# The second parts of the feed-forward weights w1 and w3, made by an adding DMA in place of a VectorE subtraction

## The chip, the core and the metric

The kernel runs on one core of one Trainium2 chip. The metric is the device time of one execution in microseconds (us). Before the change it is 2998.93 us, the median of three runs (2995.76 to 2999.79). Engines are named as the profile names them: PE is TensorE (PEld its weight loads), DVE is VectorE, ACT is ScalarE, POOL is GpSimd, SP is SyncE.

## The reference

The program computes two hybrid attention layers and then two layers of feed-forward, HGRN2 mixer with pooling, cross-attention and feed-forward, for 512 tokens of 1024 features in float32. The change touches only the feed-forward blocks, of which there are four (`ffn1` and `ffn2` of each of the two later layers). With 2816 hidden features each of them computes:

```python
def swiglu(h, w1, w3, w2):
    return (jax.nn.silu(h @ w1) * (h @ w3)) @ w2

x = x + 0.5 * swiglu(rmsnorm(x, g), w1, w3, w2)
```

## The kernel before, in words

Activations are feature-major: features on the 128 partitions, the 512 tokens on the free axis. A dense product keeps float32 accuracy with three TensorE passes. Every operand is split into a leading part of 12 significant bits (`hi`, type float32r) and the rest (`lo`), and `mm3` (lines 296 to 298) multiplies hi by hi, hi by lo and lo by hi. So every weight that comes from HBM has to be split on the chip. `chunk` does that: it loads a piece with a DMA on SP's queue into one of four buffers `wraw`, ACT copies it into `whi` (line 287, the copy rounds to float32r), and DVE writes `wlo` = piece minus `whi` (line 288). `whi` and `wlo` have two buffers each, so a chunk can be split only when the chunk two before it has been multiplied.

In `ffn`, the weights w1 and w3 lie together: a chunk holds 128 columns of w1 and 128 of w3 for all 1024 input features, 128 x 2048 elements, loaded and split in two pieces of 128 x 1024 (512 KB each). Each block runs in two halves of 11 such chunks; each half ends with 8 chunks of w2. A chunk of w1 and w3 feeds two units (banks of PSUM, three of which rotate under the name `mm`): the first is h @ w1, the second h @ w3, of 24 matmuls of 512 columns each, 48 for a chunk. `ev` evacuates them: DVE scales the first (`si`, line 886), POOL clamps it (line 501), ACT makes a sigmoid of it (lines 504 to 506), POOL multiplies (lines 888, 889), DVE multiplies the second unit with the outcome (`sb`, line 893), and ACT and DVE split that into `hh` and `hl` (lines 256, 257) for the product with w2. At the beginning of a block the row norm is worked out as well (`rt`, lines 440 to 444), which the first `si` needs.

The order of the instructions of each engine is set by the tile framework's scheduler. Every engine takes its instructions in that order, so one that waits holds back all that are behind it. `parts_of` asks for the next unit's weights ahead of the unit that is running.

Of the kernel before, what the change touches and what calls it, by code (L numbers as in the profile page):

```python
"""Two hybrid attention layers, then two HGRN2 / pool / cross-attention layers, on one core.

Activations live feature-major: features on the partitions, the 512 tokens on the free axis.
Dense products run on the tensor engine as float32r passes: an operand is split exactly into
a leading part of 12 significant bits and the rest, and three passes carry lead*lead, rest*lead
and lead*rest, which keeps the accuracy of a float32 product.
"""
# [14 lines left out]
ALU = mybir.AluOpType  # L22
# [14 lines left out]
# tiles of a tag get their room in program order, so work that runs at its own pace has a tag of its own  # L37
# [18 lines left out]
# engines of the steps that more than one can take: V(ector), P(ool), A(ctivation)  # L56
# [7 lines left out]
# ---------------------------------------------------------------- layout of the inputs (host)  # L64
def _chunks(w, c):
    """[K, M] -> [M/c, 128, K/128, c]"""
    k, m = w.shape
    return np.ascontiguousarray(w.reshape(k // P, P, m // c, c).transpose(2, 1, 0, 3))


def _cols(v):
    """[n*128] -> [128, n]"""
    return v.reshape(-1, P).T
# [37 lines left out]
def _constants():  # L111
    a = np.zeros((P, CONST.n), np.float32)

    def put(name, v):
        o, w = CONST.at[name]
        a[:, o:o + w] = v

    p = np.arange(P)[:, None]
    put("ident", np.eye(P))
    put("ones", 1.0)  # L120
    put("bd", (p // 64 == np.arange(P)[None] // 64))
    u = np.arange(512)[None]
    dist = p + 384 - u
    put("causal", np.where(dist >= 0, 0.0, BIG))
    cnt = ((dist >= 0) & (dist <= 128)) * 1 + ((dist >= 0) & (dist % 4 == 0)) * 1 + ((dist >= 0) & (dist % 16 == 0)) * 1
    put("dil", np.where(cnt > 0, -np.log(np.maximum(cnt, 1)), BIG))
    put("tri", (u >= p))
    put("reset", (u % 64 != 0))
    put("diag", p % 32 == np.arange(32)[None])
    t16 = np.arange(16)[None]  # L130
    put("pool", np.concatenate([1.0 / np.minimum(t16 + 1, w) for w in (2, 4, 8, 16)], 1))
    put("eps", EPS)
    # pairs s, t of 32 tokens in the two halves of a segment of 2 hs tokens
    lev = np.zeros((P, 5, 32), np.float32)
    s, t = np.arange(P)[:, None] % 32, np.arange(32)[None]
    for n, hs in enumerate((16, 8, 4, 2, 1)):
        lev[:, n] = (s // (2 * hs) == t // (2 * hs)) & (s % (2 * hs) < hs) & (t % (2 * hs) >= hs)
    sel = np.zeros((96, 8, P), np.float32)
    for h in range(8):
        for part in range(3):  # L140
            sel[32 * part + h, h] = 1.0
    return a, lev, sel


def _pack(i):
# [5 lines left out]
    # 8 frequencies x 16 blocks of 32 tokens  # L151
# [55 lines left out]
# ---------------------------------------------------------------- the program  # L207
class Prog:
# [9 lines left out]
    # tiles  # L218
# [34 lines left out]
    # exact split of float32 into two float32r parts  # L253
# [19 lines left out]
    def chunk(self, ap, kt, c):  # L273
        """One chunk of a weight: both parts, [128, kt, c]."""
# [7 lines left out]
        for o in range(0, n, step):  # L282
            e = min(o + step, n)
            raw = early[o // step] if early else self.raw(flat[:, o:e])
            for a in range(o, e, step // 2 if early else step):
                b = a + step // 2 if early else e
                nc.scalar.activation(hi[:, a:b], raw[:, a - o:b - o], AF.Copy)  # L287
                nc.vector.tensor_tensor(lo[:, a:b], raw[:, a - o:b - o], hi.bitcast(F32)[:, a:b], op=ALU.subtract)  # L288
# [3 lines left out]
    def mm3(self, ps, pairs, first=True, last=True):  # L292
        """ps = sum over pairs of (stationary hi, lo), (moving hi, lo)."""
# [6 lines left out]
    class Unit:  # L300
        """Work of the tensor engine in parts that other work can go between; prep loads its weights."""
# [4 lines left out]
    def weights(self, ap, kt, c):  # L306
        held = []

        def prep():
            if not held:  # L310
                held.extend(self.chunk(ap, kt, c))
# [4 lines left out]
    def unit(self, prep, kt, n, pair, evac, wait=2):  # L316
        """One bank of a dense product: the sum over kt pairs of operands."""
# [16 lines left out]
    def dense(self, chunks, kt, c, act, evac, m0=0, n=T, quick=False):  # L334
        """Feature-major product, a unit for every 128 columns of the weight (one bank); quick: the last ones evacuated at once."""
        units = []
        for ci, ap in enumerate(chunks):
            prep = self.weights(ap, kt, c)
# [8 lines left out]
    def dense_tok(self, chunks, kt, c, act, evac, nb, c0=0):  # L347
        """Token-major product: tokens on the partitions, the weight's columns on the free axis."""
# [9 lines left out]
    def later(self, n, f):  # L358
        """Run f after n more dense units."""
        self.queue.append([n, f])  # L360

    def chain(self, *steps):
        """Steps that hand over between engines, one after each dense unit, so that none waits in its queue."""
# [16 lines left out]
    def parts_of(self, units):  # L380
        """The parts of the units in order, each with its cost; the next unit's weights are loaded ahead."""
# [13 lines left out]
    def weave(self, main, fill, keep=0, lead=0):  # L395
        """Both lists in their order, merged in proportion to their cost; lead of fill's go first, keep last."""
# [14 lines left out]
    # root mean squares  # L411
    def parts(self, sq, hi, n=T, eng=None):
        """The rest of sq beside its leading part hi."""
# [4 lines left out]
    def colsum(self, ps, which, sq, n=T):  # L418
        """ps = which^T sq, which of zeros and minus ones, sq in parts."""
# [16 lines left out]
    def rsqrt(self, ps, n_mean, n=T):  # L436
        """1 / sqrt(-ps / n_mean + EPS): a table value and a Newton step."""
# [9 lines left out]
    class Next:  # L447
        """The operand of the phase after this one, built tile by tile as x gets final."""
# [39 lines left out]
    def norm(self, cur, cols=False, wait=2):  # L488
        """rstd of the tokens, emitted behind the first dense units, which need it only in their evacuation."""
# [8 lines left out]
    def sigmoid(self, x, t, clamp):  # L498
        """t = 1 / (1 + exp(-x)) as exp(-ln(1 + exp(-x))), x held above -40."""
# [10 lines left out]
    def gate(self, ps, r, then):  # L510
        """g = silu(ps * r), then(g)."""
# [5 lines left out]
    # ------------------------------------------------------------ start  # L517
# [50 lines left out]
    def setup_rope(self):  # L568
        """cos and signed sin of the angles, in a dense layout and then in their rows; reduced by multiples of 2 pi in exact parts."""
# [35 lines left out]
    # ------------------------------------------------------------ hybrid layer  # L605
    def qk_tile(self, ps, r, g, rope, done):
        """Head-wise rms norm (two heads a tile), gain, and the rotary part."""
# [33 lines left out]
    def softmax_rows(self, ps, n, mask, P_out):  # L641
        """P_out = softmax of -(ps + mask) along the free axis."""
# [8 lines left out]
    def stack(self, get, st):  # L651
        """Queries and keys of a pair of heads in parts, stacked so that one pass over 128 rows carries two products:
        [qh; qh] and [ql; ql] against [kh; kl]."""
# [18 lines left out]
    def head(self, get, st, hh, h, fox, done):  # L672
        """One head in three stages; rows 64*hh.. of the output bank get it, feature-major."""
# [6 lines left out]
        def scores(i):  # L680
            qh, ql, kk = st[hh]
            n = (i + 1) * P
            # a float32r product at full rate has at least 256 columns
# [34 lines left out]
    def pipeline(self, heads, stacks):  # L718
        """The heads' steps, those of neighbours overlapped; a pair's operands are stacked ahead of it.

        The values of a pair fill the two halves of the tensor engine's columns side by side.
        """
# [18 lines left out]
    def hybrid(self, l, cur, nx):  # L741
# [5 lines left out]
        # tiles: kb 0-3, qb 4-7, ka 8-11, qa 12-15; queries carry -1/8  # L747
# [10 lines left out]
        def ev_va(c, b, ps):  # L758
            # the first 8 columns are the forget gates
# [86 lines left out]
    def forget(self, z):  # L846
        """Running sums of the log forget gates, split into bfloat16 parts."""
# [4 lines left out]
        # log1p(e) = ln(u) + (e - (u - 1)) / u with u = 1 + e  # L852
# [19 lines left out]
    # ------------------------------------------------------------ second block  # L872
    def ffn(self, l, name, cur, nx):
# [4 lines left out]
        for half in range(2):  # L878
# [18 lines left out]
            self.go(self.dense([w13[NH * half + i] for i in range(NH)], KD, 256, xs, ev))  # L897
# [11 lines left out]
    def lower_bound(self):  # L909
        """Per channel of layer 1: lb, 1 - lb and their logs."""  # L910
# [23 lines left out]
    def hgrn_head(self, l, h, f, v, done):  # L934
        """One head as a list of steps, each ready when the one before it is through its engines.

        The decay exp(b_t - b_s), b the running sum of log f, is a product of two factors of at
        most 1 through a token between s and t: for a segment of 2 hs tokens, t in its right and
        s in its left half, that token is the left half's last. Segments of 2 .. 512 tokens
        cover every pair, and the pair t = s has no decay.  # L940
        """
# [29 lines left out]
        def bound():  # L971
            # logaddexp(log lb, log(1 - lb) + log_sigmoid(z)), k = (1 - lb) * sigmoid(-z)
# [19 lines left out]
        def q64():  # L992
            self.on("qe").tensor_tensor(g["qe"], g["qe"], f[4 + h], op=ALU.mult)
            nc.scalar.activation(g["dk"], g["dk"], AF.Exp)
            # decays of whole 64-token chunks, to the middle of 256 and of 512 tokens
# [137 lines left out]
    def mix(self, l, cur, nx):  # L1133
# [26 lines left out]
        def ev_gu(m, ps):  # L1160
# [19 lines left out]
            # the mean over the window minus the frame  # L1180
# [35 lines left out]
    def mem_kv(self, l):  # L1216
        """Keys (feature-major) and values (token-major) of the memory, as units."""
# [27 lines left out]
    def cross(self, l, cur, nx):  # L1245
# [64 lines left out]
        # the first units of the last product run between the steps of the last heads  # L1310
# [74 lines left out]
```

## Time and profile before

| | |
|---|---|
| time, median of 3 runs | 2998.93 us (2995.76 to 2999.79) |
| span of the profiled execution, first to last instruction | 2992.6 us |
| median less that span: what lies around it | 6.3 us |
| PE busy | 2929.1 us (98%) |
| DVE busy | 1674.1 us (56%) |
| ACT busy | 1406.6 us (47%) |
| POOL busy | 745.2 us (25%) |
| DMA, mean | 95 GB/s, 284.10 MB |
| granted TensorE clock, mean | 0.994 |

The profile gives busy times and the span of one execution; its time with what lies around is not listed apart, so the median of the runs stands for it. In rows of groups of instructions the columns are: line, engine, operation, output<-inputs, shapes, count | busy us, mean ns of one | idle us of the engine before them, and what ended most of that idle time. In rows of a timeline the first number is the start in us from the span's beginning, the second the duration in us; a bracket gives the idle time before and what ended it.

### The profile page before, as it was taken

The numbers are of one execution on the slowest core, as the hardware profiler recorded it, in microseconds if no ns is written. First come the engines' busy times: TensorE is split into PE (matmuls) and PEld (weight loads), VectorE is DVE, ScalarE is ACT, GpSimd is POOL, SyncE is SP. The second block draws the span as 40 slices with busy tenths as digits, with TensorE's granted clock in tenths as the row PEclk, the third lists the DMA queues.
The fourth block names the chain that finished last, engine by engine and source line by source line (L and its number), as shares of the span: only waits on it lengthen the run. The fifth ranks groups of instructions, "written<-read, shape, count | busy, mean of one in ns | idle before, by whom it ended". The sixth has DMA issues, their size and how long they took to land.

```text
span 2992.6 us, 39832 instructions
## 1 busy us (share of the span) xinstructions
PE 2929.1 (98%) x15544; PEld 2372.5 (79%) x15544; DVE 1674.1 (56%) x2698; ACT 1406.6 (47%) x2334; POOL 745.2 (25%) x613
## 2 busy tenths in 40 slices
PE   7999999999999999999999999999999999999997
PEld 6777877778788887798888888888888798888886
DVE  7976678766533337785643333433347976643333
ACT  5876467664532434464443233432434654443342
POOL 3101131011331323331032132321323330132231
PEclk9999999999999999999999999999999999999999
DMA  4432233322223232243132323223232242232322
GB/s 159 121 103 82 95 113 94 106 80 94 96 80 107 87 96 89 68 131 99 57 99 79 111 90 99 97 76 111 83 107 83 79 134 85 71 98 79 110 75 76
DMA packets 93436, 284.10 MB, mean 95 GB/s; under 512 B 12656, under 2 KB 13056, under 8 KB 93120
## 3 DMA queue, kind: packets, MB, share of 16 engines
q1 hardware_dynamic: 92928, 281.26, 29.5%
q8 instruction: 122, 2.00, 0.3%
q14 instruction: 66, 0.54, 0.1%
q10 hardware_dynamic: 288, 0.28, 0.0%
q0 software_dynamic: 32, 0.02, 0.0%
HBM read 261.46 MB, written 2.10 MB: 88 GB/s over the span
## 4 chain that ended last, share of the span: by engine, by line
PE 86%; DVE 7%; ACT 2%; issue 1%; POOL 0%; DMA 0%; DVEq 0%; ACTq 0%; POOLq 0%
PE mm L296 27%; PE mm L297 26%; PE mm L298 26%; PE po L712 2%; DVE wlo L288 1%; PE pt L701 1%; PE aux L687 1%; PE aux L421 1%; PE aux L688 1%; PE po L1103 0%; PE aux L296 0%; PE aux L298 0%; PE aux L297 0%; ACT whi L287 0%; DVE hw L1020 0%
## 5 line engine op out<-in xcount | busy, mean ns | idle before, releaser
L296 PE MATMUL mm<-xsh,whi 128*128 128x512 f32 x2304 | 926.9, 403 | 16.9 <-DVE pol L263 8.1
L297 PE MATMUL mm<-xsl,whi 128*128 128x512 f32 x2304 | 910.5, 395 | 8.0 <-DVE xsl L263 7.6
L298 PE MATMUL mm<-xsh,wlo 128*128 128x512 f32 x2304 | 911.2, 396 | 0.0
L287 ACT ACTIVATE whi<-wraw 128x1024 fp32r<-128x1024 f32 (+4 forms) x526 | 498.5, 984 | 572.2 <-PE mm L297 408.0
L288 DVE TENSOR_TENSOR wlo<-wraw,whi 128x1024 fp32r<-128x1024 f32 (+4 forms) x526 | 596.5, 1165 | 110.4 <-ACT whi L287 106.2
L296 PEld LDWEIGHTS mm<-xsh,whi 128*128 128x128 f32 x2304 | 435.6, 189 | 128.4 <-issue 13.1
L297 PEld LDWEIGHTS mm<-xsl,whi 128*128 128x128 f32 x2304 | 435.7, 189 | 108.2 <-DVE xsl L263 14.5
L298 PEld LDWEIGHTS mm<-xsh,wlo 128*128 128x128 f32 x2304 | 435.1, 189 | 101.4 <-DVE wlo L288 0.2
L501 POOL TENSOR_SCALAR sb<-si 128x512 f32<-128x512 f32 x88 | 130.8, 1487 | 770.0 <-DVE si L886 770.0
L433 POOL TENSOR_TENSOR sq<-sq,sq 128x512 f32<-128x512 f32 (+1 forms) x97 | 132.0, 1361 | 722.5 <-ACT sq L430 711.0
L893 DVE TENSOR_TENSOR sb<-mm,sb 128x512 f32<-128x512 f32 x88 | 60.9, 692 | 435.2 <-POOL sb L889 435.2
L297 PE MATMUL mm<-hl,whi 128*128 128x512 f32 x704 | 277.4, 394 | 0.0
L296 PE MATMUL mm<-hh,whi 128*128 128x512 f32 x704 | 277.2, 394 | 0.0
L298 PE MATMUL mm<-hh,wlo 128*128 128x512 f32 x704 | 276.7, 393 | 0.0
L504 ACT ACTIVATE sb<-sb 128x512 f32<-128x512 f32 x88 | 55.8, 634 | 464.1 <-POOL sb L501 464.1
L901 DVE SCALAR_TENSOR_TENSOR x<-mm,x 128x512 f32<-128x512 f32 x64 | 44.3, 692 | 306.7 <-PE mm L298 306.7
L297 PEld LDWEIGHTS mm<-hl,whi 128*128 128x128 f32 x704 | 132.3, 188 | 30.8
L296 PEld LDWEIGHTS mm<-hh,whi 128*128 128x128 f32 x704 | 131.8, 187 | 31.3
L298 PEld LDWEIGHTS mm<-hh,wlo 128*128 128x128 f32 x704 | 132.5, 188 | 30.3
L886 DVE TENSOR_TENSOR si<-mm,rt 128x512 f32<-128x512 f32 x88 | 60.9, 692 | 134.4 <-PE mm L298 134.2
L889 POOL TENSOR_TENSOR sb<-sb,si 128x512 f32<-128x512 f32 x88 | 113.9, 1296 | 67.3 <-ACT sb L506 67.3
L888 POOL TENSOR_TENSOR si<-si,rt 128x512 f32<-128x512 f32 x88 | 114.9, 1306 | 7.3
(360 smaller groups left out, 4580.8 us busy)
## 6 DMA issues: line engine op xcount, KB each, us to landing
wraw<-in_ffn_w_dram SPq DMA_DIRECT2D x176, 512.0 KB
wraw<-in_ffn_w_dram SPq DMA_DIRECT2D x64, 384.0 KB
wraw<-in_ffn_w_dram SPq DMA_DIRECT2D x64, 320.0 KB
z<-z SPq DMA_DIRECT2D x128, 128.0 KB
wraw<-in_w_out_dram SPq DMA_DIRECT2D x32, 512.0 KB
wraw<-in_w_qk_dram SPq DMA_DIRECT2D x30, 512.0 KB
wraw<-in_w_g_dram SPq DMA_DIRECT2D x16, 512.0 KB
wraw<-in_w_gate_dram SPq DMA_DIRECT2D x16, 512.0 KB
```

The costliest lines, as they stand in the source:

```text
L287: nc.scalar.activation(hi[:, a:b], raw[:, a - o:b - o], AF.Copy)
L288: nc.vector.tensor_tensor(lo[:, a:b], raw[:, a - o:b - o], hi.bitcast(F32)[:, a:b], op=ALU.subtract)
L296: self.nc.tensor.matmul(ps, ah, bh, start=first and i == 0, stop=False)
L297: self.nc.tensor.matmul(ps, ah, bl, start=False, stop=False)
L298: self.nc.tensor.matmul(ps, al, bh, start=False, stop=last and i == n - 1)
L433: (eng or self.on("acc")).tensor_tensor(acc[:, :n], acc[:, :n], sq[:, :n], op=ALU.add)
L501: clamp.tensor_scalar(t, x, -40.0, None, op0=ALU.max)
L712: nc.tensor.matmul(self.po[rows, j * P:], v[j][:, 64 * h:64 * h + 64], ptS[b][:, o:o + T - j * P], start=j == 0, stop=j == 2)
L886: nc.vector.tensor_tensor(s, ps, r["r"], op=ALU.mult)
L888: nc.gpsimd.tensor_tensor(s, s, r["r"], op=ALU.mult)
L889: nc.gpsimd.tensor_tensor(b, b, s, op=ALU.mult)
L893: nc.vector.tensor_tensor(b, ps, b, op=ALU.mult)
```

## The change

`chunk` gets a flag `added`, which `ffn` sets for its w1 and w3 chunks from the third of every half on (9 of 11). For these, ACT writes `wlo` = minus the leading part (a copy with scale -1 that rounds to float32r), a DMA issued by POOL adds the same piece of the weight from HBM to `wlo`, and ACT writes `whi` as before. The subtraction of DVE is not there for them. 4 blocks x 2 halves x 9 chunks x 2 pieces make 144 pieces. The other lines of the diff take comments and docstrings out; lines from 288 on stand five numbers later in the changed kernel.

```diff
@@ -270,8 +270,8 @@
-    def chunk(self, ap, kt, c):
+    def chunk(self, ap, kt, c, added=False):
...
@@ -284,13 +284,18 @@
             raw = early[o // step] if early else self.raw(flat[:, o:e])
             for a in range(o, e, step // 2 if early else step):
                 b = a + step // 2 if early else e
+                if added:
+                    nc.scalar.activation(lo[:, a:b], raw[:, a - o:b - o], AF.Copy, scale=-1.0)
+                    nc.gpsimd.dma_start(out=lo[:, a:b], in_=flat[:, a:b], accum_op=ALU.add)
+                    nc.scalar.activation(hi[:, a:b], raw[:, a - o:b - o], AF.Copy)
+                    continue
                 nc.scalar.activation(hi[:, a:b], raw[:, a - o:b - o], AF.Copy)
                 nc.vector.tensor_tensor(lo[:, a:b], raw[:, a - o:b - o], hi.bitcast(F32)[:, a:b], op=ALU.subtract)
...
-    def weights(self, ap, kt, c):
+    def weights(self, ap, kt, c, added=False):
...
-                held.extend(self.chunk(ap, kt, c))
+                held.extend(self.chunk(ap, kt, c, added))
...
-    def dense(self, chunks, kt, c, act, evac, m0=0, n=T, quick=False):
+    def dense(self, chunks, kt, c, act, evac, m0=0, n=T, quick=False, added=False):
...
-            prep = self.weights(ap, kt, c)
+            prep = self.weights(ap, kt, c, added and ci > 1)
...
-            self.go(self.dense([w13[NH * half + i] for i in range(NH)], KD, 256, xs, ev))
+            self.go(self.dense([w13[NH * half + i] for i in range(NH)], KD, 256, xs, ev, added=True))
```

The scheduler keeps the order of all other instructions on every engine; PE's and SP's lists are the same. Three places change.

ACT, in the middle of a half, once per chunk (`hh` is the split of the hidden features, `sb` the sigmoid of the next pair). Before:

```order
L506 ACTIVATE sb_8194<-sb_8194 128x512 [waits Activation_49]
L287 ACTIVATE whi_8232<-wraw_8234 128x1024 [waits DMAHW0_49,PE_49]
L287 ACTIVATE whi_8232<-wraw_8238 128x1024 [waits DMAHW1_49]
L256 ACTIVATE hh_8228<-sb_8194 128x512 [waits DVE_49]
L504 ACTIVATE sb_8268<-sb_8268 128x512 [waits Pool_49]
```

With the change:

```order
L511 ACTIVATE sb_8198<-sb_8198 128x512 [waits Activation_49]
L290 ACTIVATE whi_8236<-wraw_8238 128x1024 [waits DMAHW0_49,PE_49]
L288 ACTIVATE wlo_8237<-wraw_8238 128x1024 [waits DMASW2_49,DMASW1_49,PE_49]
L256 ACTIVATE hh_8232<-sb_8198 128x512 [waits DVE_49]
L288 ACTIVATE wlo_8237<-wraw_8243 128x1024 [waits DMAHW1_49]
L290 ACTIVATE whi_8236<-wraw_8243 128x1024
L509 ACTIVATE sb_8274<-sb_8274 128x512 [waits Pool_49]
```

Two copies into `wlo` are new, and `hh`, which stood behind both copies of the chunk, now stands between the two pieces.

POOL, the same place. Before:

```order
L501 TENSOR_SCALAR sb_8194<-si_8193 128x512
L888 TENSOR_TENSOR si_8193<-si_8193,rt_8039 128x512
L889 TENSOR_TENSOR sb_8194<-sb_8194,si_8193 128x512
L501 TENSOR_SCALAR sb_8268<-si_8267 128x512
```

With the change:

```order
L506 TENSOR_SCALAR sb_8198<-si_8197 128x512 [waits DMAHW7_49,DMAHW6_49,DVE_49]
L893 TENSOR_TENSOR si_8197<-si_8197,rt_8039 128x512 [waits Pool_49]
L894 TENSOR_TENSOR sb_8198<-sb_8198,si_8197 128x512 [waits Activation_49,Pool_49]
L289 DMA wlo_8237<-in_ffn_w_dram 128x1024 [waits DMASW2_49,DMASW1_49,Activation_49]
L289 DMA wlo_8237<-in_ffn_w_dram 128x1024 [waits Activation_49]
```

Both adding DMAs of a chunk stand between the last multiplication of one pair and the clamp of the next.

ACT, at the beginning of a block, where the third chunk is split and the row norm (`ry`, `rt`) is worked out. Before:

```order
L287 ACTIVATE whi_8084<-wraw_8086 128x1024 [waits DMAHW4_49,PE_49]
L440 ACTIVATE ry_8038<-aux_8031,cst_62 128x512 [waits PE_49]
L287 ACTIVATE whi_8084<-wraw_8090 128x1024 [waits DMAHW5_49]
L441 ACTIVATE ry_8038<-ry_8038 128x512 [waits Activation_49]
L442 ACTIVATE rt_8039<-ry_8038 128x512 [waits Activation_49]
```

With the change:

```order
L290 ACTIVATE whi_8084<-wraw_8086 128x1024 [waits DMAHW4_49,PE_49]
L445 ACTIVATE ry_8038<-aux_8031,cst_62 128x512 [waits PE_49]
L288 ACTIVATE wlo_8085<-wraw_8086 128x1024
L446 ACTIVATE ry_8038<-ry_8038 128x512 [waits Activation_49]
L288 ACTIVATE wlo_8085<-wraw_8091 128x1024 [waits DMAHW5_49]
L447 ACTIVATE rt_8039<-ry_8038 128x512 [waits Activation_49]
L290 ACTIVATE whi_8084<-wraw_8091 128x1024
```

Two copies of 128 x 1024 now stand ahead of the square that makes `rt`, where one stood.

## Rows read from the trace of the kernel before

**Rows 1.** The page, parts 1 and 5: engines, and weight loads of `wlo`

```profile
PE 2929.1 (98%) x15544; PEld 2372.5 (79%) x15544; DVE 1674.1 (56%) x2698; ACT 1406.6 (47%) x2334; POOL 745.2 (25%) x613
L298 PEld LDWEIGHTS mm<-xsh,wlo 128*128 128x128 f32 x2304 | 435.1, 189 | 101.4 <-DVE wlo L288 0.2
```

**Rows 2.** Two w1/w3 stretches: us, busy by engine (instructions), PEclk, DMA share, GB/s

```profile
788.00:876.00 88.00, 88.00 (x381) 71.21 (x380) 35.62 (x43) 36.13 (x49) 32.67 (x24) 1.00 0.28 89
2635.00:2724.00 89.00, 89.00 (x387) 72.37 (x386) 36.53 (x44) 37.02 (x50) 32.72 (x24) 1.00 0.28 90
```

**Rows 3.** Groups of instructions from 794 to 876 us: the two operations of a split

```profile
L288 DVE TENSOR_TENSOR wlo<-wraw,whi 128x1024 fp32r<-128x1024 f32 x14 | 16.5, 1220 | 0.0
L287 ACT ACTIVATE whi<-wraw 128x1024 fp32r<-128x1024 f32 x14 | 14.1, 1053 | 5.9 <-PE mm L297 5.9
```

**Rows 4.** Timeline of PE around the chunk that starts at 827.9 us

```profile
816.22 0.39 PE L297 MATMUL mm<-xsl,whi 128*128 128x512 f32 x1
...
828.35 0.40 PE L298 MATMUL mm<-xsh,wlo 128*128 128x512 f32 x1
...
831.15 0.40 PE L298 MATMUL mm<-xsh,wlo 128*128 128x512 f32 x1
```

**Rows 5.** Timeline of ACT and POOL in the same chunk

```profile
816.65 2.01 ACT L287 ACTIVATE whi<-wraw 128x1024 fp32r<-128x1024 f32 x2 [0.91 <-PE mm L297]
818.56 0.62 ACT L256 ACTIVATE hh<-sb 128x512 fp32r<-128x512 f32 x1
...
815.88 1.29 POOL L889 TENSOR_TENSOR sb<-sb,si 128x512 f32<-128x512 f32 x1 [0.83 <-ACT sb L506]
823.26 1.49 POOL L501 TENSOR_SCALAR sb<-si 128x512 f32<-128x512 f32 x1 [6.08 <-DVE si L886]
```

**Rows 6.** SP loads a 512 KB piece; DMA engines in the stretches behind

```profile
819.06 0.33 SPq L270 DMA_DIRECT2D wraw<-in_ffn_w_dram  x1
...
819.50:820.00 0.50, 0.50 (x4) 0.41 (x3) 0.50 (x1) 0.00 (x0) 0.00 (x0) 1.00 0.00 0
...
820.00:824.00 4.00, 4.00 (x19) 3.21 (x18) 1.46 (x3) 0.00 (x0) 0.74 (x1) 1.00 0.77 258
```

**Rows 7.** POOL's only DMA: timeline, the stretch around it, its issue (KB, us to landing)

```profile
1.66 0.76 POOL L573 DMA_DIRECT2D rope<-in_pos_dram  x1
...
3.00:7.40 4.40, 0.00 (x0) 0.00 (x0) 1.16 (x6) 2.26 (x4) 1.05 (x3) 1.00 0.95 319
...
rope<-in_pos_dram POOLq DMA_DIRECT2D x1, 16.0 KB, 5.7
```

**Rows 8.** Beginning of a block: ACT, DVE, PE; who waited for line 886

```profile
774.71 0.64 ACT L442 ACTIVATE rt<-ry 128x512 f32<-128x512 f32 x1
...
775.38 0.69 DVE L443 SCALAR_TENSOR_TENSOR rt<-aux,rt 128x512 f32<-128x512 f32 x1
776.83 0.69 DVE L886 TENSOR_TENSOR si<-mm,rt 128x512 f32<-128x512 f32 x1
...
777.66 0.42 PE L296 MATMUL mm<-xsh,whi 128*128 128x512 f32 x1
...
  PEld mm L296: 0.9, 4
```

**Rows 9.** The fourth chunk of that half: ACT, and PE at its first uses

```profile
785.35 0.63 ACT L256 ACTIVATE hh<-sb 128x512 fp32r<-128x512 f32 x1 [0.94 <-DVE sb L893]
785.88 1.99 ACT L287 ACTIVATE whi<-wraw 128x1024 fp32r<-128x1024 f32 x2
...
794.95 0.40 PE L298 MATMUL mm<-xsh,wlo 128*128 128x512 f32 x1
...
797.75 0.40 PE L298 MATMUL mm<-xsh,wlo 128*128 128x512 f32 x1
```

**Rows 10.** Two matmuls of PE 36 apart, in another chunk

```profile
850.74 0.39 PE L298 MATMUL mm<-xsh,wlo 128*128 128x512 f32 x1
...
858.98 0.39 PE L298 MATMUL mm<-xsh,wlo 128*128 128x512 f32 x1
```

## The prediction

> **What bounds the kernel now.** I read the page first. PE is busy for 2929 of the span's 2992.6 us, so time can only go where PE stands still, and only come where PE is made to [rows 1]. Next I read stretches of w1 and w3 in the first and in the last block. PE is busy in 88.00 of 88.00 us and in 89.00 of 89.00, at full granted clock, while DVE and ACT work for some 36 us each, POOL for 33, and the DMA engines for 28% [rows 2]. Then I looked for a weight load that waited for the subtraction that goes away: in the whole kernel 0.2 us [rows 1]. So DVE bounds nothing in these stretches, and what decides is whether the new way of making `wlo` is ready as early as PE asks for it.
>
> **What goes.** 144 subtractions of 1.22 us [rows 3], 176 us of DVE. PE hid all of them, but for that 0.2 us. Gain: nothing.
>
> **What ACT gets.** 144 copies of about 1.0 us (two in a row take 2.01 [rows 5]). Per chunk that makes 2 us more beside the 4.6 us that an 11.2 us chunk of ACT now holds (36.1 us of 88 [rows 2]). It fits; what counts is where the copies stand.
>
> **The adds in the middle of a half.** I follow one chunk. PE reads the last `whi` of the chunk two before at 816.22 to 816.61, and ACT starts at 816.65 [rows 4, 5]. In the new order `whi` is ready at 817.65 and minus-hi at 818.65; POOL can issue the first add. It is free: it ended its last multiplication at 817.17 and is wanted for the next clamp at 823.26 [rows 5], and an issue takes it 0.76 us [rows 7], so twice that delays no clamp. Then comes `hh` (0.62 us, its input is there by then, since it starts at 818.56 now [rows 5]), the second minus-hi ends at 820.3, and POOL issues the second add. PE asks for the first piece at 828.35 and for the second at 831.15 [rows 4].
>
> The price of an add has two terms, and the trace has neither. *Launch and landing*, without the data: the one DMA that POOL issues needs 5.7 us from issue to landing with only 16 KB, but in a stretch in which the DMA engines are 95% busy [rows 7]. The other end is an issue of 0.76 us plus the 0.95 us from SP's issue at 819.06 to the first data (none before 820.00 [rows 6]): 1.7. The queue is that of the first row, the load on the engines (28% [rows 2]) nearer to that of the second; I take the middle, 3.7. *Data*: two loads of 512 KB keep the engines busy for 0.77 x 4.00 = 3.08 us [rows 6], 1.54 for one. An add must read the weight and the old `wlo` and write one of them back. Least is 1.54; a pass each for two reads and a write would make 4.6; a second read alone makes 3.08, which I take, since a plain load is also one read and one write and is priced by one.
>
> With these the first piece lands at 818.65 + 3.7 + 3.08 = 825.4, 2.9 us ahead of need, and the second behind it at 818.65 + 3.7 + 6.16 = 828.5, 2.6 ahead. One load of a next piece between them (1.54) leaves 1.1. Even with 5.7 for the launch 0.9 and 0.6 us would be left. Cost: nothing; cover: PE's 11.2 us for the chunk between. If that cover is gone, PE waits at line 298 of every chunk (303 in the changed kernel). SP's loads into `wraw` are released by ACT's last copy of a piece instead of DVE's subtraction; they are for the chunk after the next, so a microsecond there costs nothing.
>
> The Trainium skill speaks of both terms. "Collectives: The Full Stack" (The bandwidth ceiling) says that a reducing transfer reads two sources for each write and so runs at half a copy's rate; by that an add takes 3.08 us, which is what I took, and no run here shows it yet. "DMA: Bandwidth & Descriptors" (Anatomy of one DMA, the gpsimd path) gives a fixed cost of about 2.0 us for a DMA that POOL issues. The trace shows 5.7 [rows 7], under load. By the page the pieces would be another 1.7 us early and the sum would be 3.8 us; by the row it is 12.2.
>
> **The beginning of a block.** Here one extra copy stands ahead of the square that ends at 775.35 and lets DVE start `rt` at 775.38; so `rt`, and the first `si` (776.83 to 777.52), come 1.0 us later. The first matmul of the fourth unit starts at 777.66, behind this `si`, whose bank it takes, and it is here that PE waits for line 886: 4 times, 0.9 us in all [rows 8]. The slack is nothing, and the DVE subtraction that goes frees no time, for `rt` waits for ACT. Cost: 4 x 0.95 = 3.8 us.
>
> The fourth chunk of that half is split late: ACT has `hh` at 785.35 ahead of it and begins at 785.88 [rows 9]. With `hh` up to 0.95 later, minus-hi is ready at 788.9. Pieces land at 788.9 + 3.7 + 3.08 = 795.7 and 788.9 + 3.7 + 6.16 = 798.8. PE asks at 794.95 and 797.75 [rows 9], with the bank's delay at 795.9 and 798.7: the second is 0.1 late. Cost: 4 x 0.1 = 0.4 us; with the 5.7 us launch 4 x 2.1 = 8.4. The second halves have no row norm and start like a middle chunk.
>
> **Sum.** +3.8 + 0.4 = +4.2 us on the profiled execution, whose span would be 2996.8. The span lies 6.3 us under the median of the runs, 2998.9; I add the 4.2 to that median: **3003 us**. About 0.2%, 6 us, is what a measurement of this kernel can tell from no change; so the forecast is "no change", on the slow side of it. Its own range is 2997 to 3005.
>
> **Rivals.**
>
> *The launch is near 5.7 us.* Then only the fourth chunks suffer: 4 x (0.95 + 2.1) = 12.2 us, 3011. For it: it is the only row on POOL's queue. Against: one DMA, among full engines.
>
> *The adds come late in every chunk* (slower). Place: line 298's first and fifth uses of `wlo`. Point: with the 3.7 us launch the second piece is late once an add takes over (831.15 - 822.35) / 2 = 4.4 us, with 5.7 once it takes over 3.4. Two buffers share a lateness, so half of it is lost per chunk, 72 times. With 4.6 us and the long launch it lands at 833.6, 2.4 late: 72 x 1.2 = 87 us, about 3090; at the point itself it starts from the forecast. I take 3050 as its middle. For it: nothing in this trace shows an add, and the spare time is a few us. Against: 2.6 us of spare at my prices.
>
> *The DMA engines become the bound.* Loads and adds of a chunk fill them once 3.08 + 2d exceeds 11.2, so from d = 4.1 us an add. With four passes, d = 6.2, a chunk lasts 15.4: 72 x 4.2 = 300 us, 3300. For it: the add may be worked element by element. Against: 72% of the engines' time is free now.
>
> *PE's pace* (faster). Matmuls stand 0.2333 us apart in one chunk (12 from 828.35 to 831.15 [rows 4]) and 8.24 / 36 = 0.2289 in another [rows 10]; the mean is 88.00 / 381 = 0.231 [rows 2]. If fewer DVE operations brought all 4224 matmuls of w1 and w3 to the faster pace, 4224 x 0.0021 = 9 us would be gained, some 2990 without the block's beginning. Against: the pace does not follow DVE's work in these rows.
>
> **Chances.** Forecast 0.46; long launch 0.12; late in every chunk 0.24; DMA-bound 0.13; pace 0.05. Faster by over 0.2%: 0.05. Within: 0.46. Slower: 0.12 + 0.24 + 0.13 = 0.49, spread from 3006 to 3300, so that no time in it is as likely as 3003. The range from 2990 to 3090 leaves out the DMA-bound case and a part of the pace case.
>
> **What would show it.** Right: in the middle of a half PE is still busy in all of the stretch, no wait of line 303 (298 before) for the adding DMA, DVE falls by some 176 us and ACT rises by 144, and the fourth unit of each block starts 0.9 to 1.0 us behind its predecessor's end. The DMA view gives the issue-to-landing time of the adds: 6.8 us (3.7 + 3.08) for the first, up to 8 for the second. Wrong: PE's weight loads wait for an adding DMA once or twice in each of 72 chunks; or issues on POOL that last several us and push the clamp and `hh` back.

## The result and the profile after

The changed kernel takes **3013.25 us** (median of 4 runs, 3011.18 to 3015.12) against 2997.39 us for the kernel before (4 runs, 2995.76 to 2999.79): ratio 1.0055, 95% interval 1.0042 to 1.0068. It is slower by 15.9 us. That lies inside the widest range that the prediction names, 2990 to 3090, but 10 us above the forecast of 3003, outside the forecast's own 2997 to 3005, and beyond the 0.2% that it called "no change". The profiled execution's span grew from 2992.6 to 3009.4 us, by 16.8.

The page of the changed kernel: part 1 (busy time of each engine), then DMA queues, the adds' line and the weight loads of line 303, and part 6 (KB, median us from issue to landing).

```profile
PE 2934.6 (98%) x15544; PEld 2371.4 (79%) x15544; DVE 1514.7 (50%) x2554; ACT 1542.6 (51%) x2478; POOL 870.7 (29%) x757
...
q0 software_dynamic: 20768, 75.52, 13.5%
...
L303 PEld LDWEIGHTS mm<-xsh,wlo 128*128 128x128 f32 x2304 | 435.4, 189 | 114.4 <-DMA wlo<-in_ffn_w_dram 14.5
L289 POOL DMA_DIRECT2D wlo<-in_ffn_w_dram x144 | 126.9, 883 | 201.0 <-ACT wlo L288 199.7
...
wlo<-in_ffn_w_dram POOLq DMA_DIRECT2D x144, 512.0 KB, 9.0
```

Beside [rows 1], DVE lost 159 us and ACT gained 136, a little less than costed (176 and 144), and POOL gained 126, its issues. PE has 15544 matmuls as before, and its weight loads now wait 14.5 us for the adding DMA where they had waited 0.2 us for DVE. An add lands 9.0 us after its issue; the prediction had 6.8 for the first of a chunk.

Who waited for whom, of PE's weight loads and of PE (us in total, times, longest):

```profile
PEld mm L303 <- DMA wlo<-in_ffn_w_dram: 14.5, 17, 2.8
PEld mm L301 <- DVE si L891: 4.4, 4, 1.1
PE mm L303 <- DMA wlo<-in_ffn_w_dram: 8.3, 7, 2.3
PE mm L301 <- DVE si L891: 2.7, 4, 0.7
```

Two waits, both expected in kind: the bank (line 301 for `si`), four times as in [rows 8] but longer, and the adding DMA, 17 times of 144. Where they stand is told by stretches (columns as in [rows 2]) of the first block, its two middles first:

```profile
802.00:882.00 80.00, 80.00 (x346) 64.72 (x346) 16.04 (x23) 42.46 (x54) 39.11 (x33) 1.00 0.75 175
968.00:1066.00 98.00, 98.00 (x425) 79.25 (x424) 19.50 (x28) 55.29 (x70) 50.38 (x43) 1.00 0.80 183
...
796.00:798.00 2.00, 0.00 (x1) 0.00 (x0) 0.69 (x1) 1.91 (x4) 1.04 (x2) 1.00 1.04 256
798.00:800.00 2.00, 1.67 (x4) 1.38 (x5) 0.69 (x1) 1.96 (x3) 1.23 (x2) 0.58 1.03 274
```

In the middles PE is still busy all the time at full granted clock, and its pace is what it was: 80.00 / 346 = 0.231 us a matmul. But the DMA engines went from 28% [rows 2] to 75 and 80%. From 796 to 798 PE stands still. PE's timeline there (start, duration, what ended the idle time before):

```profile
777.67 0.39 PE L303 MATMUL mm<-xsh,wlo 128*128 128x512 f32 x1
778.68 0.50 PE L301 MATMUL mm<-xsh,whi 128*128 128x512 f32 x1 [0.62 <-DVE si L891]
...
795.61 0.40 PE L302 MATMUL mm<-xsl,whi 128*128 128x512 f32 x1
798.33 0.79 PE L303 MATMUL mm<-xsh,wlo 128*128 128x512 f32 x1 [2.32 <-DMA wlo<-in_ffn_w_dram]
798.92 0.63 PE L301 MATMUL mm<-xsh,whi 128*128 128x512 f32 x1
...
801.48 0.52 PE L301 MATMUL mm<-xsh,whi 128*128 128x512 f32 x1
801.83 0.40 PE L302 MATMUL mm<-xsl,whi 128*128 128x512 f32 x1
```

The first pair is the fourth unit of the block: it starts 1.01 us behind its predecessor's start instead of 0.23, so 0.8 late. The third and fourth rows are the fourth chunk (its matmul stood at 794.95 in [rows 9]): 2.72 instead of 0.23 us apart, 2.5 late. Then matmuls follow 0.43 us apart until 801.5, with the granted clock at its lower level, 1.2 GHz (0.58 is the mean of the stretch above); the other three blocks, whose waits here are 1.1 to 1.7 us, show no such spell.

Taking every distance between the starts of two matmuls beyond 0.232 us as lost, in the four first halves: the bank 0.8 + 0.1 us in each, 3.6 together; the fourth chunk's two pieces 2.9, 2.8, 2.2 and 2.5, together 10.4; the spell of half clock 1.3. Late pieces elsewhere in the four blocks, 0.1 to 0.25 each, add about 1. That is 16.3 of the 16.8 us. The rest is differences of both signs elsewhere: at 1174 us the kernel before has a spell of the lower clock, worth 1.2 us, that the changed one lacks.

### The profile page after: what moved, and what is told of

The parts are those of the page before. It is cut to its first block, busy times and chain, and to the rows that moved or that the text cites. A ratio compares the mean times of both kernels' runs of the same rounds, so it can differ in the third digit from the quotient of the medians.

```text
span 3009.4 us, 40008 instructions
## 1 busy us (share of the span) xinstructions
PE 2934.6 (98%) x15544; PEld 2371.4 (79%) x15544; DVE 1514.7 (50%) x2554; ACT 1542.6 (51%) x2478; POOL 870.7 (29%) x757
## 3 DMA queue, kind: packets, MB, share of 16 engines
q0 software_dynamic: 20768, 75.52, 13.5%
## 4 chain that ended last, share of the span: by engine, by line
PE 83%; DVE 7%; ACT 3%; DMA 2%; POOL 1%; issue 1%; DVEq 0%; ACTq 0%; POOLq 0%; SPq 0%
PE mm L301 25%; PE mm L302 25%; PE mm L303 25%; PE po L717 2%; DMA wlo<-in_ffn_w_dram 1%; DVE wlo L293 1%; PE pt L706 1%; PE aux L692 1%; PE aux L693 1%; PE aux L426 1%; ACT wlo L288 0%; PE po L1108 0%; ACT whi L292 0%; POOL sb L506 0%; PE aux L301 0%
## 5 line engine op out<-in xcount | busy, mean ns | idle before, releaser
L292 ACT ACTIVATE whi<-wraw 128x1024 fp32r<-128x1024 f32 (+3 forms) x382 | 353.5, 958 | 494.7 <-PE mm L302 329.5
L303 PEld LDWEIGHTS mm<-xsh,wlo 128*128 128x128 f32 x2304 | 435.4, 189 | 114.4 <-DMA wlo<-in_ffn_w_dram 14.5
L293 DVE TENSOR_TENSOR wlo<-wraw,whi 128x1024 fp32r<-128x1024 f32 (+3 forms) x382 | 426.3, 1144 | 88.3 <-ACT whi L292 84.0
L290 ACT ACTIVATE whi<-wraw 128x1024 fp32r<-128x1024 f32 x144 | 151.3, 1051 | 78.2 <-PE mm L302 77.8
L289 POOL DMA_DIRECT2D wlo<-in_ffn_w_dram x144 | 126.9, 883 | 201.0 <-ACT wlo L288 199.7
```

Source lines behind the costliest of these rows:

```text
L289: nc.gpsimd.dma_start(out=lo[:, a:b], in_=flat[:, a:b], accum_op=ALU.add)
L303: self.nc.tensor.matmul(ps, al, bh, start=False, stop=last and i == n - 1)
```

## The experiments

All are made from the changed kernel, and each is compared with runs of the kernel before made beside it. In the first batch theory A says that the loss is the bank's wait and the late fourth chunk alone; in the second it has the late pieces of the middle as well. The first batch takes the fourth chunk, the third and fourth, the adds, or only the addition away.

**fourth_dve**: in the first halves chunks 3 and 4 are split by DVE as before; 128 adds are left.

```diff
-            prep = self.weights(ap, kt, c, added and ci > 1)
+            prep = self.weights(ap, kt, c, added and ci > added)
-            ... ev, added=True))
+            ... ev, added=1 if half else 3))
```

> In the first half of every block the third and the fourth chunk are split by DVE as before; the adds begin with the fifth chunk there, and with the third in the second halves (136 of the 144 pieces less 8: 128 adds stay). Theory A, the loss is the beginning of a block alone (bank wait of the fourth unit, late fourth chunk): as before the change, 2997 us, within 3; PE waits for adding DMAs less than 2 us in all. Theory B, the adds cost something in every chunk (PE's pace, contention): most of the 16 us stays, 3008 to 3012.

Measured 3000.58 us (11 runs) against 2995.78 for the kernel before: 1.0016 [1.0007, 1.0025]. Two thirds of the loss are gone, with 16 of 144 adds. Both waits shrank (PE's weight loads):

```profile
PEld mm L303 <- DMA wlo<-in_ffn_w_dram: 7.1, 19, 1.3
...
PEld mm L301 <- DVE si L891: 0.9, 4, 0.2
```

The bank's wait is back at the 0.9 of [rows 8], since the copy that stood ahead of the row norm belongs to the third chunk. What is left is 19 late pieces in the middles: 7.1 us of waiting weight loads, where theory A had under 2.

**third_dve**: only chunk 3 of the first halves goes back to DVE (`added=1 if half else 2`).

> Only the third chunk of each first half goes back to DVE (adds from the fourth chunk there). Theory A: the bank wait goes (PE at line 301 waits for si about 0.9 us in all instead of 4.4), the late fourth chunk stays, for ACT and PE both come about 1 us earlier: 3009 us, PE waits 10 to 13 us for adding DMAs. If the adds for the third chunk are what delays those of the fourth (queue), the late fourth chunk goes too: 2998 us.

3007.10 us (4 runs), 1.0040 [1.0026, 1.0053]. The bank's wait is gone, the fourth chunk stays late (0.6 to 1.7 us for its first piece, 0.8 to 1.0 more for its second). The two causes are separate. But 28 weight loads wait for adds here, 18.7 us in all, against 17 and 14.5 us in the change: more pieces of the middles are late, as in fourth_dve.

**no_add**: the adding DMA is taken out.

```diff
-                    nc.gpsimd.dma_start(out=lo[:, a:b], in_=flat[:, a:b], accum_op=ALU.add)
```

> The 144 adding DMAs are left out, all else stays; the second weight part is then only minus the leading part, so the product is another one. Theory A: only the bank wait is left, 4 x 0.85 to 0.95 us, 3001 us; no wait of the matmuls with the second weight part. Theory B, the extra ACT copies or the missing DVE work slow the chunks: more than 3005 us. A rival on the DMA side, the adds' traffic slows other things than the fourth chunk: clearly under 3001 cannot be, so the gap to 3013 is what the adds cost in all, by A 12 us.

3000.94 us (11 runs), 1.0017 [1.0009, 1.0026]. The only extra wait left is the bank's:

```profile
PEld mm L300 <- DVE si L890: 4.3, 4, 1.1
...
PE mm L300 <- DVE si L890: 2.6, 4, 0.7
```

So ACT's additional copies cost what the bank costs and nothing more that shows, and removing 144 subtractions gave nothing back.

**pool_load**: the same DMA without the addition, a plain load of the weight into `wlo`.

```diff
-                    nc.gpsimd.dma_start(out=lo[:, a:b], in_=flat[:, a:b], accum_op=ALU.add)
+                    nc.gpsimd.dma_start(out=lo[:, a:b], in_=flat[:, a:b])
```

> The adding DMA becomes a plain load of the same piece by POOL into the same buffer, so the second weight part is the whole weight and the product another one. It has one source to read instead of two. If the second read is what the data term costs (2.8 us of 16 engines an add), it falls to about 1.6, the median from issue to landing from 9.0 to between 6.5 and 8, the fourth chunk loses 1 to 2 us less per block, 3004 to 3009 us. If an add costs no more than a load and the launch is all, nothing changes: 9.0 and 3013.

3000.01 us (10 runs), 1.0016 [1.0007, 1.0025]: the time of no_add, and below the 3004 to 3009 expected. The page:

```profile
q0 software_dynamic: 20768, 75.52, 7.8%
...
wlo<-in_ffn_w_dram POOLq DMA_DIRECT2D x144, 512.0 KB, 5.8
```

It also lands earlier than the 6.5 to 8 us expected, in 5.8. The queue's share of the engines' time is 7.8% of 3001.5 us, 1.63 us a load; with the addition it is 13.5% of 3009.4, **2.82 us an add**.

The second batch changes the order and the number of adds. **pinned**: minus-hi of both pieces first, the two `whi` copies held behind them.

```diff
+        his = []
...
-                    nc.scalar.activation(hi[:, a:b], raw[:, a - o:b - o], AF.Copy)
+                    his.append((hi[:, a:b], raw[:, a - o:b - o]))
...
+        for dst, src in his:
+            self.tc.keep_in_program_order(nc.scalar.activation(dst, src, AF.Copy))
```

> All 144 adds as in the change, but ACT writes minus-hi of both pieces before the two whi, so both adds are issued one copy (1.0 us) earlier; the bank wait at the beginning of a block stays. Theory A (adds too late for the fourth chunk, and now and then by a few tenths of a us in the middle): the wait of the fourth chunk for its first piece shrinks by about 1 us per block, the few tenths in the middle vanish: 3007 to 3009 us. If lateness is not what costs (contention, pace): 3013.

3001.96 us (11 runs), 1.0019 [1.0010, 1.0028], better than expected. The bank's wait is there, the fourth chunk is almost in time:

```profile
PEld mm L304 <- DVE si L894: 5.1, 4, 1.3
PEld mm L306 <- DMA wlo<-in_ffn_w_dram: 2.8, 6, 0.9
```

One copy's time (1.04 us) does not explain this alone. Against PE's need, the fourth chunk's first add is issued that one copy earlier: at 789.66 for a matmul at 797.15, 7.5 us ahead, where the change has 6.5 (789.31 for 795.84, where the matmul would have started). But it also lands in 5.4 us instead of 9.0. I had no reason for that when it ran; the last batch gives it.

**pinned_fourth**: pinned and fourth_dve together.

> As fourth_dve (third and fourth chunk of each first half by DVE, 128 adds), with minus-hi before whi. Theory A: what was left in fourth_dve, 4.8 us, was the adds of the middle that came 0.1 to 1.0 us late; with 1.0 us more they are in time, so the time is that of the kernel before within 2 us (ratio 0.9995 to 1.0007), and PE waits under 2 us in all for adding DMAs. If the adds cost pace or other engines time: still 4 to 5 us over.

2997.53 us (11 runs), 1.0005 [0.9996, 1.0014]: not to be told from the kernel before. With 128 adds, the bank's wait is back at 0.9 us and PE's weight loads wait 0.9 us in all for adds; nothing is gained either.

**from_first**: adds for all 11 chunks of a half, 176 in all (`added and ci > 1` becomes `added`).

> Adds for all 11 chunks of every half (176 pieces). Theory A: the first two chunks of a half are split close to their use, and an add needs about 9 us where the subtraction needs 1.2, so PE waits at the beginnings of blocks: 3025 to 3045 us. Rival: before the first block DVE is on the chain that ended last, with its subtractions 22% of it from 735 to 766 us, so taking these away gives time back there: below 3013.

3029.20 us (4 runs), 1.0111 [1.0098, 1.0125]. The line that was late 17 times is late 37 times, up to 4.1 us:

```profile
PEld mm L303 <- DMA wlo<-in_ffn_w_dram: 37.7, 37, 4.1
```

In the four longest of these waits PE stands still for 2.2 to 3.7 us, each at the first piece of a block's second half, right behind w2 of the first half. Why so little of PE's work covers the add there was not followed further.

**first_two**: adds for the first two chunks of the first half of the program's first block alone, 4 in all.

```diff
-            prep = self.weights(ap, kt, c, added and ci > 1)
+            prep = self.weights(ap, kt, c, added and ci < 2)
...
-            ... ev, added=True))
+            ... ev, added=l == 0 and name == 'ffn1' and half == 0))
```

> Adds only for the first two chunks of the very first half (4 pieces in all), where DVE's subtractions are on the chain that ended last; everywhere else the kernel before. If those 7 us of DVE on the chain can be had: 2991 to 2994 us, faster than both kernels. By theory A the adds are ready 8 to 9 us after minus-hi and PE wants these chunks sooner: 2996 to 3002.

2996.50 us (11 runs), 1.0003 [0.9994, 1.0012]. At the beginning of the first block PE does wait for DVE (in the kernel before 1.6 us for line 263). That wait is gone here, but one of 0.8 us for ACT and three of 1.6 together for the adds have come in its place, so the 2991 to 2994 us hoped for did not come.

**Why 9.0 us?** At this point I held that the launch term was too small: 9.0 minus 2.82 leaves 6.2 for it, near the 5.7 of [rows 7]. The third batch cuts the data and leaves the launch. **half_add** adds 512 of each piece's 1024 columns, **eighth_add** 128, **eighth_load** loads 128 without adding.

```diff
-                    nc.gpsimd.dma_start(out=lo[:, a:b], in_=flat[:, a:b], accum_op=ALU.add)
+                    nc.gpsimd.dma_start(out=lo[:, a:a + 512], in_=flat[:, a:a + 512], accum_op=ALU.add)
```

> The change, but each add reaches over the first 512 of a piece's 1024 columns (256 KB); the other 512 columns of wlo stay minus the leading part, so half of the subtraction is left out. This tells the two terms of an add's price apart. Theory A (the launch of an adding DMA is some 6 us, its data 2.8 us for 512 KB): the median from issue to landing falls from 9.0 us by about half of the data's time, to 7.4 to 7.8. Theory B (the launch is 3.7 us as predicted, and it is the data that is slow, 5.3 us for 512 KB): it falls to 6.1 to 6.6. Time by A some 3002 to 3005 (the fourth chunk's pieces still about 1 us late), by B 3000.

> As half_add with 128 columns of each piece (64 KB); seven eighths of the subtraction are left out. Theory A: issue to landing 6.2 to 6.6 us. Theory B: 4.2 to 4.6. Time by both near 3000 (no_add's 3001), by A with a few tenths of us more per block.

> As eighth_add, but a plain load of the 128 columns without the addition (wlo holds the weight there and minus its leading part elsewhere). pool_load's 5.8 us for 512 KB, less its 1.63 us of data, would leave 4.2 us for the launch; so 4.2 to 4.5 here if only the data shrinks. If the add's launch is no longer than a plain load's, eighth_add lands equally early; if adding has a launch of its own length, eighth_add is about 2 us behind this one. Time 3000.

One run each: 3000.96, 2997.96 and 2999.45 us, beside one of 2993.81 for the kernel before; the landing is what counts here. From the page of half_add, of eighth_add (its queue as well), and of eighth_load:

```profile
wlo<-in_ffn_w_dram POOLq DMA_DIRECT2D x144, 256.0 KB, 6.5
```

```profile
q0 software_dynamic: 20768, 9.46, 2.6%
...
wlo<-in_ffn_w_dram POOLq DMA_DIRECT2D x144, 64.0 KB, 4.0
```

```profile
wlo<-in_ffn_w_dram POOLq DMA_DIRECT2D x144, 64.0 KB, 3.7
```

Theory A of this batch, a launch of 6 us, falls: a 64 KB add is there after 4.0 us, and adding has no launch of its own length (3.7 without it). Theory B, a launch of 3.7 us and slow data, has 6.1 to 6.6 us for half_add, which came, and 4.2 to 4.6 for eighth_add, a little above what came; it leaves open why the data is slow. A 64 KB add costs the engines 0.54 us (2.6% of 2996.2 us, shared by 144); with that taken off, the launch beside SP's loads is about 3.5, **near the predicted 3.7**. So 5 us of the 9.0 come with 448 KB more, though the DMA engines work only 2.82 - 0.54 = 2.3 us more on them. In the other half of that time the engines had to do something else, and SP's queue says what. The changed kernel, timeline of SP's queue and of POOL at the fourth chunk:

```profile
789.03 0.33 SPq L270 DMA_DIRECT2D wraw<-in_ffn_w_dram  x1
...
791.45 0.33 SPq L270 DMA_DIRECT2D wraw<-in_ffn_w_dram  x1
...
797.37 0.33 SPq L270 DMA_DIRECT2D wraw<-in_ffn_w_dram  x1
...
789.31 0.89 POOL L289 DMA_DIRECT2D wlo<-in_ffn_w_dram  x1 [2.33 <-ACT wlo L288]
790.78 0.86 POOL L289 DMA_DIRECT2D wlo<-in_ffn_w_dram  x1 [0.58 <-ACT wlo L288]
```

Each of ACT's copies that lets an add go also frees a `wraw` buffer, at once or one copy later, and SP refills it: with a load 0.3 us ahead of the first add and another 0.7 us behind the second. They run through the same 16 DMA engines as the adds. What each queue moved at the fourth chunk (packets, MB, share of the 16 engines' time; q1 is SP's queue, q0 POOL's), first from 789 to 792, then from 792 to 796, then from 796 to 798.3, when the first add lands:

```profile
q1 hardware_dynamic: 103, 0.40, 59.9%
```

```profile
q0 software_dynamic: 140, 0.54, 79.6%
q1 hardware_dynamic: 41, 0.12, 12.7%
```

```profile
q0 software_dynamic: 88, 0.33, 72.6%
q1 hardware_dynamic: 65, 0.27, 31.4%
```

The load of 789.03 moves 0.40 of its 0.52 MB ahead of the add's first packet and the rest beside it; a next load flies beside the add's end.

**no_raw**: added chunks load nothing into `wraw`; ACT copies a small tile that is loaded once.

```diff
+            if added:
+                if not hasattr(self, "same"):
+                    self.same = self.keep([P, 256], F32, "same")
+                    nc.sync.dma_start(out=self.same, in_=flat[:, o:o + 256])
+                src = self.same.rearrange("p (o t) -> p o t", o=1).to_broadcast((P, 4, 256))
+                part = lambda t: t[:, o:e].rearrange("p (o t) -> p o t", o=4)
+                nc.scalar.activation(part(lo), src, AF.Copy, scale=-1.0)
+                nc.gpsimd.dma_start(out=lo[:, o:e], in_=flat[:, o:e], accum_op=ALU.add)
+                nc.scalar.activation(part(hi), src, AF.Copy)
+                continue
...
```

> The change, but the chunks made by adding load nothing into wraw: both ACT copies of a piece read one small tile of 256 columns, loaded once, four times over, so whi and minus its leading part are those of that tile and not of the weight. Left out: 144 plain loads of 512 KB on SP's queue, which in the change are issued 0.3 us before a chunk's first add and 0.7 us after its second. half_add and eighth_add put the launch of an add near 3.5 us, so what makes the 9.0 us to landing is the data. Theory L (the data term of 2.8 us is right, and what I left out is that SP's loads of 1.54 us each share the DMA engines with the adds): first add 3.5 + 2.8 = 6.3 us to landing, second 3.5 + 5.6 - 1.5 = 7.7, median about 7.0; the fourth chunk's pieces land at 795.6 and 798.5 on the change's clock, in time, and the kernel takes 3000 us (bank wait alone). Theory S (an add alone is some 4 us of data, whatever runs beside it): 7.6 and 10.0 us as in the change, median near 9.0, the fourth chunk late, 3010 us.

2999.23 us (10 runs) against 2995.47: 1.0010 [1.0001, 1.0020]. The page, and the waits of PE's weight loads, in which no add is left:

```profile
q0 software_dynamic: 20768, 75.52, 14.6%
...
wlo<-in_ffn_w_dram POOLq DMA_DIRECT2D x144, 512.0 KB, 6.5
```

```profile
PEld mm L306 <- DVE si L896: 4.5, 4, 1.1
```

The same 144 adds of 512 KB land in 6.5 us instead of 9.0, and not one is late. They are issued at the same places: the fourth chunk's first at 791.47 for a matmul at 798.01, 6.5 us ahead as in the change, for all of this execution runs 2.2 us later there. Theory L holds, with a landing a little earlier than its 7.0; theory S (an add is slow by itself) falls: 2.5 us of the 9.0 are the loads. At the fourth chunk they are more: its two adds land 5.4 and 6.4 us after their issue here, and 9.0 and 10.9 in the change. The engines' time for an add did not fall (14.6% of 3000.2 us is 3.04 each), so it is the queueing behind the loads that went, not work of the add. The stretches show it: in the change the engines are at 0.88 or more from 790 on, when the fourth chunk's adds are issued (789.31, 790.78); without the loads they are idle until 792, half a microsecond after the first issue (791.47), and at half again from 798, behind the first landing (791.47 + 5.4 = 796.9). The changed kernel first, then no_raw (columns as before):

```profile
790.00:792.00 2.00, 2.00 (x11) 1.63 (x10) 0.85 (x2) 1.43 (x2) 1.42 (x3) 1.00 0.89 199
792.00:794.00 2.00, 2.00 (x11) 1.63 (x10) 0.00 (x0) 0.76 (x2) 1.92 (x2) 1.00 0.88 158
794.00:796.00 2.00, 2.00 (x9) 1.31 (x7) 0.00 (x0) 1.89 (x3) 1.16 (x2) 1.00 0.97 172
```

```profile
790.00:792.00 2.00, 2.00 (x10) 1.67 (x9) 0.87 (x2) 2.00 (x4) 0.53 (x1) 1.00 0.00 0
792.00:794.00 2.00, 2.00 (x10) 1.63 (x10) 1.02 (x2) 1.59 (x2) 1.42 (x3) 1.00 0.55 51
794.00:796.00 2.00, 2.00 (x11) 1.63 (x10) 0.00 (x0) 0.63 (x1) 1.92 (x2) 1.00 1.03 199
796.00:798.00 2.00, 2.00 (x10) 1.63 (x9) 0.00 (x0) 1.86 (x4) 1.15 (x2) 1.00 1.01 190
798.00:800.00 2.00, 2.00 (x10) 1.63 (x9) 0.69 (x1) 1.89 (x3) 1.05 (x2) 1.00 0.47 92
```

It also fits pinned: there the loads wait for the copies held behind both adds, and SP issues its load at the fourth chunk only at 792.33, 2.67 us after the first add, which then lands in the 5.4 us that no_raw has too. What was not tried is to hold SP's loads back in the changed kernel and leave all else as it is.

## Why the prediction was right and wrong

**What bounds, what goes, what ACT gets**: right. No stretch of PE's work got faster when 144 subtractions went, and the copies fit beside the rest; no_add shows both.

**The beginning of a block, the bank**: right. 4 x 0.95 was forecast, 0.8 + 0.1 in each block came, and third_dve shows that the cause is the third chunk's copy ahead of the row norm.

**The launch, 3.7 us**: near, by eighth_add (about 3.5, beside SP's loads). The row on POOL's queue, 5.7 [rows 7], was the misleading end. **The data, 3.08 us**: near as the engines' work, 2.82 by the queue's share. The Trainium skill, "Collectives: The Full Stack" (The bandwidth ceiling), has a reducing transfer at half a copy's rate. By that an add would cost two plain loads; here it costs 2.82 / 1.63 = 1.7 of the same queue, so the rule is near and a little dear. For an add without loads beside it the two terms together, 6.8, are even too much: the first of no_raw's fourth chunk lands in 5.4, which leaves 2.6 for its launch.

**The failing step is the sum of these two at the fourth chunk**: "Pieces land at 788.9 + 3.7 + 3.08 = 795.7 and 788.9 + 3.7 + 6.16 = 798.8". They landed at 789.31 + 9.0 = 798.3 and 790.78 + 10.9 = 801.7, and 4 x 0.1 us became 10.4 and a spell at half clock. The start was right (minus-hi ended at 789.0), both terms were near, and the sum had no term for the plain loads that the same copies release. What they are worth there, no_raw tells: 8.98 - 5.42 = 3.6 us for the first add and 10.87 - 6.43 = 4.4 for the second. I had looked at those loads and asked only whether *they* could be late ("they are for the chunk after the next, so a microsecond there costs nothing"), and I put one load of 1.54 us between the adds in the middle of a half but none at the fourth chunk, where there was no spare time at all. At the 1.54 us of [rows 6], one load ahead of the first piece (issued at 789.03) and two ahead of the second (that one and the one of 791.45) would have given 795.7 + 1.54 = 797.2 and 798.8 + 3.08 = 801.9, where 798.3 and 801.7 were measured. This count of loads was made behind the result, and it leaves 1.1 us of the first piece open. The Trainium skill has the rule, "DMA: Bandwidth & Descriptors" (Queues, rings and completion order): each DMA engine takes turns between the queues that have work for it. That both queues' packets run side by side agrees (31.4% and 72.6% of the engines' time from 796 to 798.3). Even turns are not shown: from 793.5 to 796 the loads' queue moves next to nothing (0.00 MB), though a load was issued at 791.45.

**The adds in the middle**: nearly right. 2.9 and 2.6 us of spare were forecast, less 1.5 for a load; in fact most pieces come in time and a few 0.1 us late. How little is left shows in fourth_dve: 19 of its weight loads wait, up to 1.3 us.

**The rivals**: "The launch is near 5.7" gave 3011 and the measured time is 3013, but it is not what happened: the delay at the fourth chunk is of that size (2.6 for its 2.1), its cause is another one. A time that fits a rival is not yet that rival. That 3013 lies between 2990 and 3090 is no merit of the sum either: the range reaches so far because of "late in every chunk". That rival did not come; its point, an add of 4.4 us, was not reached by one of 2.82. The DMA engines are no bound at 75 to 80%. PE's pace did not change.

## What to carry to other kernels

When a DMA is put in a place where a buffer comes free, list what else that same release starts: a refill of the buffer runs through the same engines, and the new transfer lands later by it. Price the new transfer as launch, data and the transfers that fly beside it, and at the place with the least spare time first; the mean share of the DMA engines (28% before) says nothing about the microseconds behind one release. Work taken from an engine that nobody waits for gave nothing back here (no_add).

## What the runs showed of the hardware that I had not expected

- Adding has no launch of its own: 64 KB land in 4.0 us with the addition and in 3.7 without it. But POOL is held longer: the median issue is 0.90 us with it (eighth_add) and 0.57 without (eighth_load). The prediction took 0.76 from its one row [rows 7].
- The adds' landing spreads widely with what flies beside them: 6.3 to 11.6 us in the changed kernel, 5.3 to 8.9 in no_raw.
- A standstill of PE was sometimes followed by a spell of the lower clock, and sometimes not. After PE had stood still for 2.3 us from 796.0, the granted clock was at its lower level, 1.2 GHz, until about 801.7, and every matmul took twice its distance: 1.3 us on top of the 2.5 that the piece was late. The pieces late by 1.1 to 1.7 us at the same place of the other blocks were not followed by that. In from_first matmuls also come 0.43 us apart behind a wait of 2.3 us. Yet at another place of the program, where PE stands still for 3.2 us in both kernels, such a spell follows in the kernel before (granted clock 0.50 from 1174 to 1176) and none in the changed one (1.00 from 1178 to 1182). The kernel before first:

```profile
1173.48 0.66 PE L1074 MATMUL aux<-hW 128*32 128x32 f32 x32 [3.16 <-ACT ha L232]
```

```profile
1178.82 0.46 PE L1079 MATMUL aux<-hW 128*32 128x32 f32 x32 [3.15 <-ACT ha L232]
```
